# Stick-breaking attention: where a pair's queries are split, and how the query products are spread over the heads

## The chip, the cores and the metric

The kernel runs on one core of a Trainium2 chip. The metric is the device time in microseconds (us) of one execution. Five engines work from queues of their own, each strictly in the order in which the program lists its instructions: TensorE (PE, matrix products; its weight loads are shown as PEld), VectorE (DVE), ScalarE (ACT), GpSimd (POOL) and SyncE (SP), whose queue here issues the DMAs. Semaphores connect them: an instruction at the head of a queue waits for its inputs, and everything behind it on that queue waits too.

## The reference, cut to what matters

Two small transformer blocks run one after the other on 512 tokens of width 1024. The change touches only the attention of the second block, with 16 heads of 64 features:

```
q = split_heads(u @ attn_w_q[i])
o = stick_breaking_attention(q, k_shared, v_shared)
h = h + o @ attn_w_o[i]
...
z = einsum('bhqd,bhkd->bhqk', qb, kb) * scale
log_one_minus = where(causal, log_sigmoid(-z), 0)
log_remain = cumsum(log_one_minus, reverse) - log_one_minus
weights = where(causal, exp(log_sigmoid(z) + log_remain), 0)
out = einsum('bhqk,bhkd->bhqd', weights, vb)
```

## The kernel before, in words

All activations lie transposed, features on the partitions. A float32 product is made of three products of rounded halves (`mm3`): high by high, high by low, low by high. So every operand is split first: ScalarE (or VectorE) copies it into the rounded high half, VectorE subtracts that from the operand to get the low half.

The second block's attention is `stick()`. Two heads share 128 partitions, so heads go in eight pairs p = h // 2. The queries of pair p are one product of eight steps with a column block of `attn_w_q_2`; `q_out` scales the finished product into the tile `raw[p]` on VectorE (line 1272). `q_split` (lines 1282 to 1298) makes two stacked operands of it, one for each head: two copies on ScalarE (line 1287), two subtractions on VectorE (line 1294), and, as each operand holds its half once in each half of the partitions, four DMAs on SP's queue that copy 64 partitions to the other 64: the two high halves (line 1291), then the two low halves (line 1298). `k_split` (lines 1300 to 1306) does the keys with two ScalarE copies and two VectorE subtractions, without DMA.

For each head the work runs in this order. `scores` (L1318, mask L1322) multiplies keys by both query halves into PSUM, in the blocks B (768 columns, three key tiles) and A (512 columns, one key tile). ScalarE makes |z|, exp and ln of B and |z| and exp of A in `head_a` (lines 1327, 1328, 1331), and the ln of A in `head_b`. VectorE makes the softplus, adds up key tiles and splits it (`soft`, lines 1336 to 1342). TensorE adds the reversed cumulative sums into the same PSUM banks (`remain`, L1353: ten products for B, four for A), ScalarE takes the exponential of that (`weights`, L1360), and once for each pair `values` multiplies by the values (L594), whose result `y_split` splits on ScalarE (L275) and VectorE (L278).

The loop over h is pipelined by one head: iteration h issues `head_a(h + 1)`, that is the scores and the first functions of the next head, then `remain` and `weights` of head h. The two PSUM tiles of scores rotate, so `scores(h + 2)` waits for `weights(h)`.

Between these, `fill(n)` issues n steps of a generator `work()`: 39 steps of three 512-column products each. Step 1 is also where `raw[3]` is written. Steps 1 to 32 are the query products of pairs 4 to 7, eight steps each, all into one PSUM bank `wb`; with the last of its eight steps each issues its `q_out`, and the first step of the next one has to wait for that `q_out` to have read the bank. Steps 33 to 39 are the first seven steps of the output projection, which read y[0] to y[6] in turn. `FILL[h]` steps stand between `scores(h + 1)` and `remain(h)`, `FILL2[h]` steps at the end of iteration h, just ahead of `scores(h + 2)` in TensorE's queue. `self.ahead()`, also near the end of an iteration, splits the next weight block (ScalarE L214, VectorE L221) where the step before has taken one, and after every second block the next 1 MB weight load follows on SP's queue (L170).

Of the kernel before, what the change touches and what calls it, by code (L numbers as in the profile page):

```python
# [17 lines left out]
KT = 8  # L18
# [7 lines left out]
SQ = 4  # L26
PC = 3
COPIES = ("dada", "davv")
FILL = (1, 1, 1, 1, 0, 1, 1, 1, 1, 2, 1, 1, 0, 2, 1, 0)
FILL2 = (2, 1, 1, 2, 1, 3, 1, 3, 0, 2, 1, 3, 1, 2, 0, 3)  # L30
DUP = lambda nc: nc.vector.tensor_copy
KCUT = (0, 3, 6, 8)
CLIP = 256
# [62 lines left out]
class Kernel:  # L96
# [1161 lines left out]
    def stick(self):  # L1258
# [16 lines left out]
        def stacked(n):  # L1275
            return [self.tile("u", F32R) for _ in range(n)]

        def side(i):

            return slice(64 * i, 64 * i + 64), slice(64 - 64 * i, 128 - 64 * i)  # L1280

        def q_split(p, q):

            hi, lo = qs[p] = stacked(2), stacked(2)
            for i in range(2):
                r, other = side(i)
                nc.scalar.copy(hi[i][r], q[r])
                if p == 0:
                    nc.vector.tensor_copy(out=hi[i][other], in_=q[r])
                else:  # L1290
                    nc.sync.dma_start(hi[i][other].bitcast(F32), hi[i][r].bitcast(F32))
            for i in range(2):
                r, other = side(i)
                nc.vector.tensor_tensor(out=lo[i][r], in0=q[r], in1=hi[i][r].bitcast(F32), op=ALU.subtract)
                if p == 0:
                    nc.vector.tensor_tensor(out=lo[i][other], in0=q[r], in1=hi[i][r].bitcast(F32), op=ALU.subtract)
                else:
                    nc.sync.dma_start(lo[i][other].bitcast(F32), lo[i][r].bitcast(F32))

        def k_split(p):  # L1300

            ks[p] = stacked(2)
            for i in range(2):
                r, other = side(i)
                nc.scalar.copy(ks[p][i][r], self.K[p][r])
                nc.vector.tensor_tensor(out=ks[p][i][other], in0=self.K[p][r], in1=ks[p][i][r].bitcast(F32), op=ALU.subtract)
# [37 lines left out]
        def remain(h, ts):  # L1344

            o = z[h, len(ts)]
            own = [(t, t, self.tri) for t in ts]
            later = [(t + 1, t, self.rest if t > 0 else self.ones) for t in ts if t < 3]
            hi, lo = parts[h]
            for s, ops in ((hi, own), (hi, later), (lo, later), (lo, own)):  # L1350
                for t2, t, m in ops:
                    n, e = S - P * t2, OFF[S - P * t] + S - P * t - (S if t > 0 else 0)
                    nc.tensor.matmul(o[:, e - n : e], lhsT=m, rhs=s[:, OFF[n] : OFF[n] + n],  # L1353
                                     start=False, stop=s is lo and t2 == t, skip_group_check=True)

        def weights(h, c):
            if h not in wt:
                wt[h] = self.tile("b")
            n = c.stop - c.start
            nc.scalar.activation(wt[h][:, c], z[h, 1 if c is A else 3][:, 0:n], AF.Exp)  # L1360

        def head_a(h):

            sps[h] = self.tile("b")
            parts[h] = (self.tile("b", F32R), self.tile("b", F32R))
            scores(h, (1, 2, 3))
            scores(h, (0,))
            exps(h, B, z[h, 3][:, 0:768])
            ln(h, B)
            exps(h, A, z[h, 1])  # L1370

        def head_b(h):
            soft(h, B, z[h, 3][:, 0:768])
            ln(h, A)
            soft(h, A, z[h, 1])

        def values(p):
            self.pair_values(self.V[p], (wt.pop(2 * p), wt.pop(2 * p + 1)), vb)

        def y_split(p):  # L1380
            y[p] = self.split(vb)
# [7 lines left out]
        raw = {}  # L1389
# [34 lines left out]
        def fill(n):  # L1424
            for _ in range(n):
                next(steps, None)

        for h in range(NH):
            p = h // 2
            if h % 2 == 0 and 0 < p < KT - 1:  # L1430
                q_split(p + 1, raw.pop(p + 1))
                k_split(p + 1)
            if h + 1 < NH:
                head_a(h + 1)
            fill(FILL[h])
            remain(h, (1, 2, 3))
            remain(h, (0,))
            weights(h, B)
            if h + 1 < NH:
                head_b(h + 1)  # L1440
            weights(h, A)
            if h % 2 == 0 and p > 0:
                values(p - 1)
                y_split(p - 1)
            self.ahead()
            fill(FILL2[h])
            if h == NH - 2:
                ob = self.part(2)
                outs += [ob[:, 0:S], ob[:, S : 2 * S]]
                ws.append(self.take("attn_w_o_2", 1))  # L1450
                self.proj(outs[1], ws[1], y, 0, 6)
# [170 lines left out]
```

## Time and profile before

| | us |
|---|---|
| median of 3 runs | 2487.1 (2486.02 to 2488.62) |
| the profiled execution's own time | 2485.29 |
| its span, first to last instruction | 2483.5 |
| mean granted TensorE clock | 0.995 of full speed |
| stick(), from the first split of queries to the last steps of its first three output columns (1941.6 to 2083.6 in the span) | 142.0 |

The profiled execution is 1.81 us below the median of the runs, and 1.79 us of it lie outside the span. Rows of the timeline give the start and the length in us, the engine, the line of the kernel, the operation, the tile written and the tiles read, and, in brackets, how long the engine had been idle before and what released it. Entries are merged when they follow each other on one line; "x6" is six instructions.

### The profile page before, as it was taken

How to read it: one execution, taken by the hardware profiler on the slowest of the kernel's cores; microseconds unless marked ns; L12 is line 12 of the kernel's file. 1: busy time of each engine (PE TensorE's matmuls, PEld its weight loads, DVE VectorE, ACT ScalarE, POOL GpSimd, SP SyncE). 2: the span in 40 equal slices, each digit the busy share in tenths (PEclk: the TensorE clock that was granted, in tenths of full speed). 3: DMA queues.
4: the chain of work that ended last, by engine and by line, in shares of the span. 5: the costliest groups of instructions: out<-in, count | busy, mean ns of one | idle time of the engine just before them, and what ended most of it. 6: DMA issues, size and time to landing. Idle time of an engine off the chain costs nothing.

```text
span 2483.5 us, 29340 instructions
## 1 busy us (share of the span) xinstructions
PE 2442.0 (98%) x12060; PEld 2022.5 (81%) x12060; DVE 1364.6 (55%) x1917; ACT 911.0 (37%) x1298; POOL 173.9 (7%) x160
## 2 busy tenths in 40 slices
PE   8999999999999999899999999999999999999998
PEld 7887889877888886588888888888888777888887
DVE  7767575865443447874443444344445796444343
ACT  5335332553222335552222332222223795322232
POOL 2200110020000010330000010000001001000001
PEclk9999999999999999999999999999999999999999
DMA  4332323213223222313223222222222221322321
GB/s 171 96 114 82 106 104 120 90 69 110 96 97 113 85 102 89 96 54 106 94 97 113 85 102 99 93 94 102 94 102 85 72 73 51 106 94 100 113 85 68
DMA packets 51829, 237.42 MB, mean 96 GB/s; under 512 B 13168, under 2 KB 15600, under 8 KB 29808
## 3 DMA queue, kind: packets, MB, share of 16 engines
q1 hardware_dynamic: 51696, 235.55, 27.3%
q8 instruction: 95, 1.56, 0.3%
q14 instruction: 38, 0.31, 0.0%
HBM read 225.67 MB, written 2.13 MB: 92 GB/s over the span
## 4 chain that ended last, share of the span: by engine, by line
PE 86%; DVE 6%; ACT 3%; DMA 3%; issue 1%; POOL 0%; SPq 0%; DVEq 0%; ACTq 0%; POOLq 0%
PE bg L259 15%; PE bg L260 14%; PE bg L261 14%; PE mm L259 11%; PE mm L261 11%; PE mm L260 11%; DVE wl L221 2%; DMA d<-s 1%; PE part L259 1%; PE part L260 1%; PE part L261 1%; PE mm L594 1%; PE mm L1009 1%; DMA u<-d 1%; PE bg L576 1%
## 5 line engine op out<-in xcount | busy, mean ns | idle before, releaser
L221 DVE TENSOR_TENSOR wl<-raw,wh 128x1024 fp32r<-128x1024 f32 (+1 forms) x406 | 495.0, 1245 | 176.1 <-ACT wh L214 173.4
L259 PE MATMUL bg<-xg,wh 128*128 128x512 f32 x1440 | 562.0, 390 | 6.9 <-ACT wh L198 4.6
L260 PE MATMUL bg<-xg,wh 128*128 128x512 f32 x1440 | 560.8, 389 | 0.5 <-DVE xg L286 0.5
L261 PE MATMUL bg<-xg,wl 128*128 128x512 f32 x1440 | 560.9, 389 | 0.3 <-DVE wl L199 0.3
L214 ACT CAST wh<-raw 128x1024 fp32r<-128x1024 f32 (+1 forms) x406 | 403.1, 1029 | 398.4 <-PE mm L260 215.4
L259 PEld LDWEIGHTS bg<-xg,wh 128*128 128x128 f32 x1440 | 270.7, 188 | 64.7 <-ACT wh L198 5.1
L260 PEld LDWEIGHTS bg<-xg,wh 128*128 128x128 f32 x1440 | 270.7, 188 | 57.1 <-DVE xg L286 1.0
L261 PEld LDWEIGHTS bg<-xg,wl 128*128 128x128 f32 x1440 | 270.5, 188 | 56.9 <-DVE wl L199 0.7
L873 DVE TENSOR_TENSOR u<-bg,u 128x512 f32<-128x512 f32 x88 | 60.8, 691 | 381.6 <-PE bg L261 361.4
L874 ACT ACTIVATE u<-u 128x512 f32<-128x512 f32 x88 | 55.7, 633 | 560.0 <-DVE u L873 560.0
L259 PE MATMUL mm<-b,wh 128*128 128x512 f32 (+1 forms) x672 | 260.6, 388 | 0.0
L261 PE MATMUL mm<-b,wl 128*128 128x512 f32 (+1 forms) x672 | 260.6, 388 | 0.0
L260 PE MATMUL mm<-b,wh 128*128 128x512 f32 (+1 forms) x672 | 260.6, 388 | 0.0
L300 POOL TENSOR_TENSOR u<-u,u 128x512 f32<-128x512 f32 x61 | 82.7, 1360 | 1794.1 <-ACT u L298 1793.6
L464 DVE SCALAR_TENSOR_TENSOR x<-mm,x 128x512 f32<-128x512 f32 x111 | 76.5, 689 | 210.6 <-PE mm L261 210.6
L259 PE MATMUL mm<-xg,wh 128*128 128x512 f32 x400 | 159.7, 399 | 1.5 <-ACT b L1328 1.3
L261 PE MATMUL mm<-xg,wl 128*128 128x512 f32 x400 | 156.3, 391 | 0.0
L260 PE MATMUL mm<-xg,wh 128*128 128x512 f32 x400 | 156.3, 391 | 0.0
L259 PEld LDWEIGHTS mm<-b,wh 128*128 128x128 f32 x672 | 126.2, 188 | 25.9
L260 PEld LDWEIGHTS mm<-b,wh 128*128 128x128 f32 x672 | 126.2, 188 | 25.9
L261 PEld LDWEIGHTS mm<-b,wl 128*128 128x128 f32 x672 | 126.1, 188 | 25.8
L259 PE MATMUL mm<-u,wh 128*128 128x512 f32 x248 | 97.6, 394 | 0.6 <-DVE u L1236 0.6
(255 smaller groups left out, 3442.0 us busy)
## 6 DMA issues: line engine op xcount, KB each, us to landing
raw<-w SPq DMA_DIRECT2D x171, 1024.0 KB, 4.8
raw<-w SPq DMA_DIRECT2D x32, 896.0 KB, 4.6
b<-dec SPq DMA_DIRECT2D x8, 640.0 KB, 7.1
u<-relb SPq DMA_DIRECT2D x16, 256.0 KB, 5.1
u<-d SPq DMA_DIRECT2D x14, 256.0 KB, 5.9
u<-u SPq DMA_DIRECT2D x28, 128.0 KB, 2.2
b<-b SPq DMA_DIRECT2D x32, 66.0 KB, 2.0
x<-x SPq DMA_DIRECT2D x8, 256.0 KB, 5.6
```

The source lines that it names most:

```text
L214: nc.scalar.copy(hi[:, s], raw[:, s])
L221: self.nc.vector.tensor_tensor(out=lo[:, s], in0=raw[:, s], in1=hi[:, s].bitcast(F32), op=ALU.subtract)
L259: nc.tensor.matmul(out, lhsT=a[0], rhs=b[0], start=start, stop=False)
L260: nc.tensor.matmul(out, lhsT=a[0], rhs=b[1], start=False, stop=False)
L261: nc.tensor.matmul(out, lhsT=a[1], rhs=b[0], start=False, stop=stop)
L300: eng.tensor_tensor(out=acc, in0=acc, in1=sq, op=ALU.add)
L464: nc.vector.scalar_tensor_tensor(out=x, in0=ps, scalar=scale, in1=x, op0=ALU.mult, op1=ALU.add)
L576: self.nc.tensor.transpose(o[:, d0 : d0 + P], p[:, s0 : s0 + P], self.ident)
L594: self.nc.tensor.matmul(o[r, P * t : S], lhsT=v[:, t, r], rhs=pt[i][:, OFF[n] : OFF[n] + n], start=t == 0, stop=t == 3)
L873: nc.vector.tensor_tensor(out=a, in0=o[:, 0:S], in1=self.rb, op=ALU.mult)
L874: nc.scalar.activation(a, a, AF.Silu)
L1009: nc.tensor.matmul(o[32 * g : 32 * g + 32], lhsT=d[j + g], rhs=q[g][:, x0 : x0 + t.stop - t.start], start=j == 0, stop=j == n - 4)
```

## The change

`q_split` of the next pair moves, in the iterations of heads 2, 4, ..., 12, from the start of the iteration to a place behind `weights(h, A)` of that iteration, ahead of `values` and `y_split`. And the two lists that spread the steps of `work()` over the heads get other numbers.

```
-FILL = (1, 1, 1, 1, 0, 1, 1, 1, 1, 2, 1, 1, 0, 2, 1, 0)
-FILL2 = (2, 1, 1, 2, 1, 3, 1, 3, 0, 2, 1, 3, 1, 2, 0, 3)
+FILL = (1, 1, 1, 1, 0, 1, 1, 1, 1, 2, 1, 1, 0, 2, 0, 0)
+FILL2 = (3, 2, 2, 2, 1, 3, 1, 3, 1, 3, 0, 0, 1, 2, 1, 3)
...
         for h in range(NH):
             p = h // 2
             if h % 2 == 0 and 0 < p < KT - 1:
-                q_split(p + 1, raw.pop(p + 1))
                 k_split(p + 1)
             if h + 1 < NH:
                 head_a(h + 1)
...
                 head_b(h + 1)
             weights(h, A)
+            if h % 2 == 0 and 0 < p < KT - 1:
+                q_split(p + 1, raw.pop(p + 1))
             if h % 2 == 0 and p > 0:
                 values(p - 1)
                 y_split(p - 1)
```

Counted from the lists, the steps that end a query product (8, 16, 24, 32) fall before into `FILL` of head 3, `FILL` of head 6, `FILL` of head 9 and `FILL2` of head 11; after, into `FILL` of head 2, `FILL2` of head 5 (its first of three), `FILL2` of head 7 (its last) and `FILL` of head 10. Step 39, the one that reads y[6], falls before into `FILL2` of head 15; after, into `FILL2` of head 14.

## Rows read from the trace of the kernel before

**Rows 1.** The page's first part: busy time of TensorE in the whole span.
```profile
PE 2442.0 (98%) x12060; PEld 2022.5 (81%) x12060; DVE 1364.6 (55%) x1917; ACT 911.0 (37%) x1298; POOL 173.9 (7%) x160
```

**Rows 2.** Windows of stick(): length, busy time of each engine, granted clock, DMA.
```profile
core 0: us, PE busy (x) PEld busy (x) DVE busy (x) ACT busy (x) POOL busy (x), PEclk, DMA share, GB/s
1963.20:2039.90 76.70, 74.60 (x445) 59.31 (x445) 72.51 (x115) 75.12 (x116) 0.00 (x0) 1.00 0.19 50
...
2053.00:2056.00 3.00, 3.00 (x9) 2.41 (x9) 2.50 (x5) 2.78 (x4) 0.00 (x0) 0.54 0.00 0
```

**Rows 3.** ScalarE's timeline in stick(); L1327 on 768 columns opens a head.
```profile
1963.22 0.81 ACT L1327 ACTIVATE b<-part 128x768 f32<-128x768 f32 x1 [2.11 <-PE part L1322]
...
1971.10 0.81 ACT L1327 ACTIVATE b<-part 128x768 f32<-128x768 f32 x1
...
1972.82 0.84 ACT L1331 ACTIVATE b<-b 128x768 f32<-128x768 f32 x1
...
1976.95 0.81 ACT L1327 ACTIVATE b<-part 128x768 f32<-128x768 f32 x1
...
1982.27 1.25 ACT L1287 CAST u<-u 64x512 fp32r<-64x512 f32 x2
...
1984.83 0.81 ACT L1327 ACTIVATE b<-part 128x768 f32<-128x768 f32 x1
...
1990.60 1.07 ACT L214 CAST wh<-raw 128x1024 fp32r<-128x1024 f32 x1
...
2044.44 1.26 ACT L1287 CAST u<-u 64x512 fp32r<-64x512 f32 x2 [4.36 <-DVE u L1272]
...
2053.16 0.81 ACT L1327 ACTIVATE b<-part 128x768 f32<-128x768 f32 x1 [0.26 <-PE part L1322]
...
2061.00 0.82 ACT L1327 ACTIVATE b<-part 128x768 f32<-128x768 f32 x1 [0.57 <-PE part L1322]
...
2072.22 1.46 ACT L1360 ACTIVATE b<-part 128x768 f32<-128x768 f32 x2 [4.93 <-PE part L1353]
```

**Rows 4.** VectorE's timeline: softplus, a pair's splits, a scaled query product.
```profile
1973.72 0.96 DVE L1336 SCALAR_TENSOR_TENSOR b<-part,b 128x768 f32<-128x768 f32 x1
...
1978.76 0.68 DVE L278 TENSOR_TENSOR u<-mm,u 128x512 fp32r<-128x512 f32 x1
...
1984.98 1.40 DVE L1294 TENSOR_TENSOR u<-u,u 64x512 fp32r<-64x512 f32 x2
...
2043.72 0.68 DVE L1272 SCALAR_TENSOR_TENSOR u<-mm,u 128x512 f32<-128x512 f32 x1
```

**Rows 5.** TensorE's timeline: scores, steps of the generator, cumulative sums, values.
```profile
1962.00 0.85 PE L1318 MATMUL part<-u,u 128*128 128x384 f32 x5 [0.36 <-DMA u<-u]
...
2003.27 0.50 PE L259 MATMUL mm<-xg,wh 128*128 128x512 f32 x1 [0.16 <-DVE u L1272]
...
2051.47 1.02 PE L1318 MATMUL part<-u,u 128*128 128x384 f32 x6 [3.91 <-ACT b L1360]
...
2056.26 2.24 PE L1353 MATMUL part<-b,c 128*128 128x384 f32 x14
...
2059.71 0.92 PE L1318 MATMUL part<-u,u 128*128 128x384 f32 x6
...
2062.12 2.24 PE L1353 MATMUL part<-b,c 128*128 128x384 f32 x14
...
2066.59 0.50 PE L259 MATMUL part<-u,wh 128*128 128x512 f32 x1
...
2070.82 2.23 PE L1353 MATMUL part<-b,c 128*128 128x384 f32 x14
...
2074.35 2.37 PE L594 MATMUL mm<-b,u 128*64 128x512 f32 x16
```

**Rows 6.** SP's queue, and issue to landing of the low query halves' copies.
```profile
1971.60 1.41 SPq L1298 DMA_DIRECT2D u<-u x2
...
DMA to landing us min/median/max: 2.2/2.2/6.0
```

More of the change, by code (lines that the diff above doesn't have):

```diff
@@ L28 @@
 COPIES = ("dada", "davv")
-FILL = (1, 1, 1, 1, 0, 1, 1, 1, 1, 2, 1, 1, 0, 2, 1, 0)
-FILL2 = (2, 1, 1, 2, 1, 3, 1, 3, 0, 2, 1, 3, 1, 2, 0, 3)
+FILL = (1, 1, 1, 1, 0, 1, 1, 1, 1, 2, 1, 1, 0, 2, 0, 0)
+FILL2 = (3, 2, 2, 2, 1, 3, 1, 3, 1, 3, 0, 0, 1, 2, 1, 3)
 DUP = lambda nc: nc.vector.tensor_copy
@@ L1430, in stick @@
             if h % 2 == 0 and 0 < p < KT - 1:
-                q_split(p + 1, raw.pop(p + 1))
                 k_split(p + 1)
@@ L1441, in stick @@
             weights(h, A)
+            if h % 2 == 0 and 0 < p < KT - 1:
+                q_split(p + 1, raw.pop(p + 1))
             if h % 2 == 0 and p > 0:
```

## The prediction

> **What bounds the kernel now.** The first thing read is the page's busy times [rows 1]: TensorE 98% of the span. That is true of the feed-forward stages and says nothing about this one, so the next view is the windows of stick() alone. From 1963.20 to 2039.90, the part in which the loop runs evenly, TensorE has work in 74.60 of 76.70 us, but ScalarE in 75.12 and VectorE in 72.51 [rows 2]. Three engines are full at once, and the timelines say which of them leads. On ScalarE the first |z| of head 3 starts at 1971.10, of head 4 at 1976.95, of head 5 at 1984.83 [rows 3], and in this stretch no entry of ScalarE follows idle time. The short interval (5.85 us) leads from an odd head to the next pair's even one, the long one (7.88 us) from an even head to its odd partner; in the long one ScalarE also has the two query copies (1.25 us, at 1982.27) and the two key copies. So ScalarE's instruction count sets the pace, with hardly any slack around it. A wait put in front of a |z| is paid in full: ScalarE has nothing else that it may do, since its queue is in order.
>
> One wait is already there: at 2044.44 the query copies of the last pair begin after 4.36 us of idle ScalarE, released by `q_out` (L1272) [rows 3], which stands on VectorE at 2043.72 [rows 4]. Step 32 ends that pair's product only in `FILL2` of head 11, so its `q_out` is queued behind the whole softplus of head 12.
>
> **What is removed.** After the change step 32 falls into `FILL` of head 10, and `q_split` no longer stands ahead of the odd head's |z|. The 4.36 us go. And each long interval that holds a `q_split` loses its 1.25 us of copies: 7.88 becomes about 6.62. No instruction is removed: ScalarE copies, VectorE subtractions, the 24 DMAs of six moved splits and 39 steps are all issued still, in other places.
>
> **What the moved split waits for.** This is the term that decides. The operands that `q_split(p + 1)` makes in iteration 2p are read by `scores(2p + 2)`, the first thing TensorE does in iteration 2p + 1. Before, the split stood a whole head earlier. Now its low halves stand on VectorE behind `soft(2p + 1)`, and must then go through SP's queue. From the |z| of the odd head to the |z| of the next even head the chain is:
> - |z|, exp, ln of B on ScalarE, to VectorE's first softplus instruction: 1971.10 to 1973.72, 2.62 us [rows 3, 4];
> - the softplus of both blocks, to the instruction behind it: 1973.72 to 1978.76, 5.04 us [rows 4];
> - the first of the two low-half subtractions: half of 1.40, 0.70 us [rows 4];
> - its DMA: SP issued the two low copies of an earlier pair from 1971.60, and such a copy lands 2.2 us (median) after its issue [rows 6];
> - from the landing to the |z|: the score products released by that DMA went at 1962.00, and the |z| of that head began at 1963.22 [rows 5, 3], 1.22 us.
>
> Sum 11.78 us, where the short interval was 5.85. The high half is no later: its copies follow `weights(h, A)` on ScalarE, while VectorE is still in the softplus. The lower bound of the DMA is 2.2 and the upper 6.0, the longest row, which a copy took that followed a 1 MB weight load. By the lists the load that comes near a split is issued in iteration 8, behind the low copies, so I take 2.2.
>
> **What the moved steps wait for.** Step 16 ends the product of pair 5. Its `q_out` is now issued in `FILL2` of head 5, behind `soft(6)`, and steps 17 and 18 stand directly behind it and ahead of `scores(7)`. Step 17 must wait for that `q_out`. The trace of before shows this wait in small (0.16 us at 2003.27 [rows 5]). From |z| of head 6 to |z| of head 7 it makes 2.62 + 5.04 + 0.68 (`q_out`) + 1.41 (two steps of 0.705, from the six between 2066.59 and 2070.82 [rows 5]) + 1.29 (scores at 2059.71 to |z| at 2061.00 [rows 5, 3]) = 11.04 us in place of 6.62. At step 25 (ahead of the cumulative sums of head 8) the wait is for work that these sums need too; it is taken at nothing, and at 0.7, one `q_out`, in the range. The extra steps in heads 0 to 2 lie where TensorE waited for DMA or weights anyway; if that cover is gone they cost 0.7 each.
>
> **The weight copies** (1.07 us each [rows 3]) fall by the new steps into iterations 3, 6, 8, 11. In 6 and 8 the new wait of the |z| hides them; in 3 and 11 they add to the intervals of heads 5 and 13.
>
> **The sum over heads 2 to 15.** Before: |z| of head 2 at 1963.22, of head 15 at 2061.00 [rows 3], 97.78 us. After: six short intervals of 11.78 (70.7) and seven long ones: six of 6.62, two of them with 1.07 more, and one of 11.04 (52.9). 123.6 us, so +25.8. It contains the gone 4.36.
>
> **The tail.** Step 39 reads y[6] and now stands in iteration 14, ahead of six output steps and of `remain(15)`. y[6]'s low half is queued behind `soft(15)`: |z| of head 15 + 2.62 + 5.04 + 0.68 = 8.34, then seven steps (4.94) and 1.40 from the cumulative sums to the weights (2070.82 to 2072.22) = 14.68 us, where it was 11.22 [rows 3, 5]: +3.46. Step 39 no longer stands between these sums and the last values; weights ended at 2073.68 (2072.22 + 1.46) and the values started at 2074.35 [rows 3, 5], so 0.67 comes back: +2.8.
>
> **The clock.** After its only long wait (3.91 us, at 2051.47) TensorE ran at a granted 0.54 from 2053 to 2056 [rows 5, 2], the lower level of 1.2 GHz for nearly all of it. Scores and two steps then took 4.79 us (to 2056.26) against 2.41 + 0.70 at the full clock (2059.71 to 2062.12, plus a step): 1.68 us, of which the |z| saw 0.40 (1.69, 2051.47 to 2053.16, against 1.29). By the chain above two new TensorE waits are as long, ahead of `scores(6)` (4.3 us) and of step 17 (4.4); I charge 0.40 for the first and 1.68 for the second, where steps stand ahead of the scores. The wait at head 14 exists before as after. +2.1.
>
> **Sum:** 25.8 + 2.8 + 2.1 = +30.7. Against the profiled execution's 2485.29 that is 2516.0; the median of the runs lies 1.81 higher, so 2518.
>
> **Rivals.**
> 1. *The clock falls after every new wait.* The waits ahead of scores 4, 8, 10, 12, of step 25 and of step 39 are 1 to 3.4 us by the same walk. Each would cost 0.40 to 1.68 more: +2.4 to +10.1, up to 2528. Against it: in the even part TensorE was idle for 2.10 us in all (76.70 - 74.60), and the granted clock stayed at 1.00 [rows 2]. The Trainium skill ("TensorE: Matmul & The Clock Gate", "HAM oscillation") says that in a loop whose matmul bursts are parted by waits the array falls to half rate again in every round. By that rule this rival's 2528 holds, by the row above 2518.
> 2. *Only the split costs.* If `q_out` of pair 5 and y[6] come early enough, the step moves are free: 4.4, 2.8 and 1.7 drop out, 2509. VectorE would have to run the softplus out of the list's order; nothing in the trace does.
> 3. *Faster.* The split is in time: the copies' 1.25 us only pass from the long interval to the short one (5.85 + 1.25 = 7.10), and the gone 4.36 us are the whole effect: 2482.7, with the tail's 2.8 still 2485.5. It decides from the point where the low half lands within 7.10 - 1.22 = 5.9 us of the odd head's |z|. The chain needs 11.78 - 1.22 = 10.6 to there; the 5.04 us of softplus ahead of the subtraction would have to be out of it. The list puts them in.
> 4. *No effect*, should the list not be the order of the queues. In the trace all queues follow it.
>
> **How the numbers follow.** 0.74 for the forecast (2510 to 2525), 0.12 for rival 1, 0.08 for rival 2, 0.04 for rival 3, 0.02 for rival 4. The unknown ends are the clock (+10), the DMA (+3.8 for one late copy) and, downwards, waits that overlap. The range that leaves out no more than 2 in 10 is 2505 to 2529. About 0.2% (5 us) is what a measurement can tell from no change; the first three cases are all slower by more: 0.94, same 0.03, faster 0.03.
>
> **What would show it.** In the profile after: a wait of ScalarE of 3.5 to 5 us ahead of the |z| of heads 4, 6, 8, 10, 12 and 14, ended by TensorE's scores, and these ended by a DMA; no idle time ahead of the last pair's query copies; a wait of 4 us for `q_out` ahead of step 17; `remain(15)` 3 us later after the last |z|. If the |z| of even heads still follow the odd ones by about 6 us, the chain is wrong and with it the sum.

## The result and the profile after

The changed kernel takes 2529.49 us (median of 4 runs, 2528.95 to 2531.24), the kernel before 2487.84: ratio 1.0171, 95% interval 1.0159 to 1.0183. It is slower by 41.7 us; 30.2 were forecast (2518 against the 2487.8 of before), and the time lies just beyond the upper end of the range, 2529.

The profiled execution took 2528.95 us, 43.7 more than the one of before. The windows of the loop, first from |z| of head 3 to |z| of head 15, then around the wait and the work of head 6:

```profile
core 0: us, PE busy (x) PEld busy (x) DVE busy (x) ACT busy (x) POOL busy (x), PEclk, DMA share, GB/s
1970.70:2099.80 129.10, 99.01 (x499) 78.56 (x498) 87.12 (x136) 84.18 (x128) 0.00 (x0) 0.84 0.15 41
...
2000.00:2003.20 3.20, 0.41 (x1) 0.19 (x1) 2.26 (x4) 0.00 (x0) 0.00 (x0) 0.82 0.55 126
2003.20:2005.40 2.20, 2.16 (x9) 2.19 (x10) 0.00 (x0) 0.08 (x1) 0.00 (x0) 0.50 0.10 23
2005.40:2009.60 4.20, 4.20 (x17) 3.72 (x17) 1.61 (x3) 3.57 (x6) 0.00 (x0) 0.59 0.00 0
2009.60:2016.50 6.90, 4.29 (x23) 3.46 (x23) 5.28 (x9) 2.92 (x6) 0.00 (x0) 1.00 0.00 0
```

Three engines were full in this loop before [rows 2]; now ScalarE works 84 of 129 us. And the granted clock, 0.98 before from head 3 to head 15, is 0.84 over the loop: the scores of head 6 run at 0.50, the lower level. So do those of the other five even heads:

```profile
1982.00:1984.10 2.10, 2.10 (x9) 2.10 (x10) 0.00 (x0) 0.07 (x1) 0.00 (x0) 0.50 0.03 8
2027.20:2029.40 2.20, 2.16 (x9) 2.19 (x10) 0.18 (x1) 0.08 (x1) 0.00 (x0) 0.50 0.02 5
2048.20:2050.30 2.10, 2.09 (x9) 2.10 (x10) 0.21 (x1) 0.01 (x1) 0.00 (x0) 0.50 0.56 115
2069.70:2071.80 2.10, 2.10 (x9) 2.10 (x10) 0.00 (x0) 0.02 (x1) 0.00 (x0) 0.50 0.05 13
2090.20:2092.30 2.10, 2.08 (x9) 2.10 (x10) 0.00 (x0) 0.00 (x0) 0.00 (x0) 0.50 0.03 7
```

ScalarE's timeline:

```profile
1970.67 0.81 ACT L1327 ACTIVATE b<-part 128x768 f32<-128x768 f32 x1
...
1984.03 0.81 ACT L1327 ACTIVATE b<-part 128x768 f32<-128x768 f32 x1 [6.19 <-PE part L1322]
...
1992.57 0.81 ACT L1327 ACTIVATE b<-part 128x768 f32<-128x768 f32 x1
...
2005.32 0.81 ACT L1327 ACTIVATE b<-part 128x768 f32<-128x768 f32 x1 [5.58 <-PE part L1322]
...
2016.48 0.81 ACT L1327 ACTIVATE b<-part 128x768 f32<-128x768 f32 x1 [3.96 <-PE part L1322]
...
2084.61 1.25 ACT L1287 CAST u<-u 64x512 fp32r<-64x512 f32 x2
...
2099.81 0.81 ACT L1327 ACTIVATE b<-part 128x768 f32<-128x768 f32 x1 [1.51 <-PE part L1322]
...
2115.68 1.46 ACT L1360 ACTIVATE b<-part 128x768 f32<-128x768 f32 x2 [9.98 <-PE part L1353]
```

Heads 3 to 4 take 13.36 us where it was 5.85, heads 5 to 6 12.75; head 6 to 7, the interval with step 17, 11.16. ScalarE's waits ahead of the six even heads are 4.5 to 6.2 us, somewhat longer than the 3.5 to 5 that were to show the chain. The last pair's query copies (2084.61) wait for nothing now. Who holds the scores back stands first on TensorE's timeline of the changed kernel:

```profile
1978.96 0.41 PE L1318 MATMUL part<-u,u 128*128 128x384 f32 x1 [1.75 <-DMA u<-u]
1981.95 1.41 PE L1318 MATMUL part<-u,u 128*128 128x384 f32 x5 [2.58 <-DMA u<-u]
...
2000.82 0.41 PE L1318 MATMUL part<-u,u 128*128 128x384 f32 x1 [3.01 <-DMA u<-u]
2003.24 1.40 PE L1318 MATMUL part<-u,u 128*128 128x384 f32 x5 [2.01 <-DMA u<-u]
...
2013.69 0.50 PE L259 MATMUL mm<-xg,wh 128*128 128x512 f32 x1 [2.61 <-DVE u L1272]
```

The copies that released the scores of head 6, on SP's queue, the high halves (L1291) and the low (L1298):

```profile
1998.52 1.10 SPq L1291 DMA_DIRECT2D u<-u  x2
2000.94 1.15 SPq L1298 DMA_DIRECT2D u<-u  x2
```

And what stood ahead of these low halves on VectorE, from the first softplus instruction of head 5 on:

```profile
1995.17 0.96 DVE L1336 SCALAR_TENSOR_TENSOR b<-part,b 128x768 f32<-128x768 f32 x1 [0.71 <-ACT b L1331]
...
2000.20 1.40 DVE L1294 TENSOR_TENSOR u<-u,u 64x512 fp32r<-64x512 f32 x2
```

For head 6 the chain reads: |z| of head 5 at 1992.57, softplus at 1995.17 (2.60 later), low halves at 2000.20 (5.03), issue at 2000.94 (0.74), scores released at 2003.24 (2.30), |z| at 2005.32 (2.08). Four of the five terms are those of the forecast to within 0.1 us. The last was put at 1.22. And TensorE waits twice within one set of scores: first for the high halves' copy, then, one product later, for the low halves': 3.01 + 2.01 us.

Summed over all heads (from the starts of L1327 on 768 columns; the last column is the |z| of head 15 to `weights(15)`):

| kernel | six short intervals | seven long ones | head 2 to 15 | tail |
|---|---|---|---|---|
| before | 37.20 | 60.58 | 97.78 | 11.22 |
| forecast, without its 2.1 of clock | 70.7 | 52.9 | 123.6 | 14.68 |
| after | 77.54 | 58.19 | 135.73 | 15.87 |

Of the 43.7 us in the profile, 37.95 lie between heads 2 and 15, 4.65 in the tail up to the weights, and 0.86 ahead of head 2, 0.75 of them already ahead of head 0, where nothing was moved.

### The profile page after: what moved, and what is told of

Its sections match the earlier page's. It is cut to its first block, busy times and chain, and to the rows that moved or that the text cites. A ratio compares the mean times of both kernels' runs of the same rounds, so it can differ in the third digit from the quotient of the medians.

```text
span 2527.2 us, 29361 instructions
## 1 busy us (share of the span) xinstructions
PE 2460.0 (97%) x12060; PEld 2037.2 (81%) x12060; DVE 1365.8 (54%) x1917; ACT 911.5 (36%) x1298; POOL 174.0 (7%) x160
## 4 chain that ended last, share of the span: by engine, by line
PE 87%; DVE 6%; ACT 3%; DMA 3%; issue 2%; POOL 0%; SPq 0%; DVEq 0%; ACTq 0%; POOLq 0%
PE bg L259 15%; PE bg L260 15%; PE bg L261 15%; PE mm L259 11%; PE mm L260 11%; PE mm L261 11%; DVE wl L221 1%; PE part L259 1%; PE part L260 1%; PE part L261 1%; PE part L1318 1%; DMA u<-u 1%; PE mm L1009 1%; DMA d<-s 1%; PE bg L576 1%
```

## The experiments

The theory after this reading: the chain and the step waits are as forecast, and what is missing is a TensorE clock that falls in all six waits, not in one. The rival: the chain itself is longer than its rows, or the two lists cost more than was worked out.

**The two parts alone.** e1_move has the new place of the split and the old lists, e2_lists the new lists and the old place.

```
e1_move:  -                q_split(p + 1, raw.pop(p + 1))      (start of iteration)
          +                q_split(p + 1, raw.pop(p + 1))      (behind weights(h, A))
e2_lists: -FILL = ... -FILL2 = ...   +FILL = ... +FILL2 = ...  (as in the change)
```

> Only the move of the split; the two lists as before. If the low halves' chain (ScalarE 2.6, softplus 5.0, subtraction 0.7, DMA 2.2, scores 1.2 us) and a TensorE clock that falls in each of the six waits are the cause, the six intervals from an odd head's |z| to the next even head's are 12.5 to 13 us as in the changed kernel, and the time is about 2520 (2488 + 22.6 of waits + some 10 of clock). If the lists carry most of the loss, the time stays under 2500.

> Only the two lists; the split stands where it stood before. By the chain for step 17 (4.4 us), the tail (2.8) and the gone 4.36 us wait: 2491 to 2496, short intervals still about 6 us. If the lists carry most of the loss: over 2510.

e1_move: 2522.04 us, ratio 1.0129 (1.0112 to 1.0146), +32.9 on its 2489.19. Its short intervals are 12.74 to 12.88 us. e2_lists: 2500.67 us, ratio 1.0047 (1.0032 to 1.0062), +11.5. So the move is most of the loss, and the two add up to 44.4 where both together cost 41.7. The lists alone cost more than the 2 to 7 us expected. The largest single piece of the excess is a wait that the changed kernel doesn't have: heads 5 to 6 take 10.17 us where it was 6.71. The tail is 16.05 us where 14.68 were forecast, and heads 7 to 8 and 9 to 10 take 1.8 and 2.0 more than before. In e2_lists, TensorE's timeline at the scores of head 6 and at step 17:

```profile
1997.00 2.12 PE L1318 MATMUL part<-u,u 128*128 128x384 f32 x6 [4.49 <-DMA u<-u]
...
2008.16 0.50 PE L259 MATMUL mm<-xg,wh 128*128 128x512 f32 x1 [3.34 <-DVE u L1272]
```

And SP's queue in e2_lists ahead of that, with the weight load (L170):

```profile
1989.66 0.33 SPq L170 DMA_DIRECT2D raw<-w  x1
1990.10 1.10 SPq L1291 DMA_DIRECT2D u<-u  x2
1991.29 1.21 SPq L1298 DMA_DIRECT2D u<-u  x2
```

The lists move a weight load into the end of iteration 3. With the split in its old place, at the start of iteration 4, the copies are issued 0.44 us behind that 1 MB, and TensorE waits 4.49 us for them ahead of the scores of head 6. In the changed kernel the split stands a head later: there the load was issued at 1993.05 and the first copy at 1998.52.

**The clock, held up.** e3_warm is the changed kernel with idle products ahead of the six scores; e6_move_warm is the same on e1_move; e8_warm17 adds 16 ahead of step 17.

```
+WARM = {4: 16, 6: 18, 8: 14, 10: 14, 12: 18, 14: 22}
+            for _ in range(WARM.get(h, 0) if len(ts) == 3 else 0):
+                nc.tensor.matmul(o[:, 0:S], lhsT=self.identr, rhs=k, start=True, stop=True, ...)
e8_warm17, ahead of step 17:
+                        for _ in range(16):
+                            nc.tensor.matmul(vb, lhsT=self.identr, rhs=ks[3][0], start=True, stop=True)
```

> The changed kernel with 14 to 22 more products of 512 columns ahead of the scores of heads 4, 6, ..., 14; they write the bank that the scores then start anew, so nothing is computed from them, and they only keep TensorE at work during its wait. Clock theory (a clock fallen to half in all six waits carries what the forecast missed): granted clock 1.00 in those scores, short intervals near 11.8 in place of 12.8, long ones shorter too, time 2515 to 2521. Rival (the DMA or the queues are slower than the rows said): intervals as in the changed kernel, 2529 or more.

> Only the move, with the idle products of e3_warm ahead of the six scores (they compute nothing). Clock theory: short intervals 11.9 to 12.5, from head 2 to head 15 about 121 us where the move alone has 131; time some 10 us under the move alone (2522), about 2511. Rival (the clock matters only where the lists add waits): within 3 us of the move alone.

> e3_warm with 16 more idle products ahead of step 17, into the bank of the values, which the values start anew. Clock theory: the interval from head 6 to head 7 falls from 12.7 to 11.0 us, as the forecast's chain has it without the clock, and the time by 1.5 to 2 us. Rival (that interval's wait is something else): it stays at 12.7.

e3_warm: 2525.06 us, ratio 1.0142 (1.0127 to 1.0157); e6_move_warm: 2513.00 us, ratio 1.0094 (1.0078 to 1.0109); e8_warm17: 2522.50 us, ratio 1.0129 (1.0116 to 1.0143). The scores of head 4 in e3_warm, by windows:

```profile
1981.95:1984.10 2.15, 2.15 (x14) 1.98 (x15) 0.00 (x0) 0.93 (x2) 0.00 (x0) 1.00 0.06 13
```

TensorE's timeline of e3_warm around them (L1317 the idle products, L1321 the scores):

```profile
1977.05 3.89 PE L1317 MATMUL part<-u,c 128*128 128x512 f32 x16
1980.78 0.34 PE L1321 MATMUL part<-u,u 128*128 128x384 f32 x1
1981.95 0.82 PE L1321 MATMUL part<-u,u 128*128 128x384 f32 x5 [0.83 <-DMA u<-u]
```

The release by the DMA comes at 1981.95, as without the idle products, but the five score products take 0.82 us in place of 1.41, at a granted 1.00. The adding of work to a waiting engine made the kernel faster:

| kernel | short | long | head 2 to 15 | tail |
|---|---|---|---|---|
| e1_move | 76.79 | 54.42 | 131.21 | 11.22 |
| e6_move_warm | 72.79 | 47.08 | 119.87 | 11.22 |
| after | 77.54 | 58.19 | 135.73 | 15.87 |
| e3_warm | 72.97 | 54.75 | 127.72 | 16.04 |
| e8_warm17 | 72.99 | 53.89 | 126.88 | 14.46 |

The granted clock over the loop of e1_move and of e6_move_warm:

```profile
1970.00:2100.00 130.00, 104.22 (x529) 83.55 (x529) 90.78 (x142) 89.61 (x137) 0.00 (x0) 0.84 0.15 41
1978.00:2090.00 112.00, 105.96 (x598) 85.20 (x594) 83.53 (x130) 82.46 (x127) 0.00 (x0) 1.00 0.18 48
```

In the loops of the profiled executions the clock is 11.3 us of the move alone (1.9 for each of six waits) and 8.0 of the changed kernel; in the medians of the whole time it is 9.0 and 4.4. e3_warm's expectation of 2515 to 2521 was missed by 4 us, for two reasons. Its interval from head 6 to 7 grew from 11.16 to 12.72, since TensorE now waited 4.31 us ahead of step 17 and the clock fell there. And its profiled execution gives 2.8 us back behind the attention: from `weights(15)` to the end it takes 414.4 us, the changed kernel 411.5, with a TensorE wait of 2.25 us at 2170.91 where the changed kernel has 0.96. What lengthens that wait the runs don't show.

TensorE at step 17, in e3_warm and in e8_warm17:

```profile
2011.12 0.58 PE L260 MATMUL mm<-xg,wh 128*128 128x512 f32 x1 [4.31 <-DVE u L1273]
...
2015.12 0.40 PE L260 MATMUL mm<-xg,wh 128*128 128x512 f32 x1
```

e8_warm17 fills that wait too and has 11.82 from head 6 to 7, where 11.0 were expected. The 16 products ran on to 2015.12, where `q_out` had ended at 2014.30, and that is the 0.8 between. Its time is 2.6 us under e3_warm's, more than the 1.5 to 2 expected, but not for the reason given: in the profiled executions the loop is only 0.8 us shorter; the tail, which the 16 products do not touch, is 1.6 shorter (see the last section).

**The chain ahead of the low halves.** e4_between is the changed kernel with the split between the softplus of B and that of A; e9_high_early leaves the high halves' copies and DMAs at the start of the iteration and moves only the low halves.

```
e4_between, in the place of head_b(h + 1):
+                soft(h + 1, B, z[h + 1, 3][:, 0:768])
+                if h % 2 == 0 and 0 < p < KT - 1:
+                    q_split(p + 1, raw.pop(p + 1))
+                ln(h + 1, A)
+                soft(h + 1, A, z[h + 1, 1])
e9_high_early:
+                q_high(p + 1, raw[p + 1])           (start of iteration, ahead of k_split)
...
-                q_split(p + 1, raw.pop(p + 1))
+                q_low(p + 1, raw.pop(p + 1))        (behind weights(h, A))
```

> The changed kernel with the split issued between the softplus of block B and that of block A of the next head, so that 1.8 us of softplus leave the chain ahead of the low halves. If VectorE's order decides: each of the six short intervals 1.8 us shorter, time about 2519. Rival (the ScalarE copies or the high halves' DMA decide): no change, 2529.

> The changed kernel with the high halves (ScalarE copies and their DMAs) issued where they stood before, and only the low halves' subtractions and DMAs in the new place. If the chain through the softplus to the low halves decides: short intervals 12.5 to 13 us as in the changed kernel, the long ones 1.25 us longer, time 2530 to 2537. Rival (the high halves' copies and DMAs, for which TensorE waits first, decide): short intervals fall by 2 us or more, time under 2520.

e4_between: 2517.99 us, ratio 1.0120 (1.0102 to 1.0139). Its six short intervals sum to 65.96 against 77.54, 1.93 less each, where 1.8 of softplus had left the chain. But this edit also brings the high halves forward (their first copy is issued at 1975.13 where it was 1976.62), so it does not part the low halves from the high ones. e9_high_early does: 2536.87 us, ratio 1.0186 (1.0172 to 1.0200). Its short intervals (76.52) are those of the changed kernel, though the high halves went out a head earlier; the long ones grew by 6.6 in sum. TensorE's timeline at the scores of head 4 (L1327 is the line of the scores in this kernel) shows the first product without a wait and all of it ahead of the second:

```profile
1981.60 0.33 PE L1327 MATMUL part<-u,u 128*128 128x384 f32 x1
1987.18 1.41 PE L1327 MATMUL part<-u,u 128*128 128x384 f32 x5 [5.25 <-DMA u<-u]
```

So the low halves behind the softplus decide, and the high halves, for which TensorE waits first, do not.

**The wait that the change was rid of, alone.** e5_step32 is the kernel before, the split in its old place, with step 32 ahead of the softplus of head 12.

```
-FILL = (1, 1, 1, 1, 0, 1, 1, 1, 1, 2, 1, 1, 0, 2, 1, 0)
-FILL2 = (2, 1, 1, 2, 1, 3, 1, 3, 0, 2, 1, 3, 1, 2, 0, 3)
+FILL = (1, 1, 1, 1, 0, 1, 1, 1, 1, 2, 1, 2, 0, 2, 1, 0)
+FILL2 = (2, 1, 1, 2, 1, 3, 1, 3, 0, 3, 2, 0, 1, 2, 0, 3)
```

> The kernel before with steps 30 to 32 a little earlier (one more step in FILL of head 11, in FILL2 of heads 9 and 10, none in FILL2 of head 11), the split left in its old place. Theory: the 4.36 us wait of ScalarE ahead of the last pair's query copies goes, and with it the one fall of the clock; 2483 to 2485 where before has 2488. Rival: TensorE's own work fills the end of the stage, so the wait only moves there and the time stays.

2484.81 us against 2489.99, ratio 0.9976 (0.9966 to 0.9985): 5.2 us faster than before, and faster than the changed kernel. The windows of e5_step32, all of stick() and the place where the wait was:

```profile
1941.60:2083.00 141.40, 136.02 (x776) 107.63 (x775) 121.34 (x189) 117.37 (x179) 0.00 (x0) 1.00 0.20 58
2035.00:2060.00 25.00, 24.30 (x146) 18.91 (x145) 24.06 (x40) 23.47 (x36) 0.00 (x0) 1.00 0.25 72
```

The interval from head 12 to 13, 12.37 us with the wait, is 7.88, and the clock stays at 1.00. From head 2 to 15 it takes 93.10 us where it was 97.78.

## Why the prediction was right in its direction and short in its size

- **The chain to the low halves** was right, term by term (2.60, 5.03, 0.74, 2.30 against 2.62, 5.04, 0.70, 2.2). With the clock held up, the short intervals are 11.85 to 12.55 us where 11.78 was forecast. In the changed kernel the 0.6 more of heads 3 to 4 has a row: a `q_out` (0.69 us, at 1973.27) stands ahead of that softplus. The 2.1 us that six such intervals run over in e6_move_warm are small beside the rest; where they come from was not followed up.
- **The gone wait** was right: 4.36 us, and e5_step32 shows what it is worth by itself, with the one fall of the clock: 5.2 us, 4.7 of them between heads 2 and 15.
- **Step 17** was right as a chain, 11.04 forecast, 11.02 measured when the overrun of 0.8 is taken off e8_warm17's 11.82. In the changed kernel TensorE, still slow from head 6, reached it late and waited only 2.61 us, not 4.4, and the clock did not fall there: the 1.68 charged for it was not paid. e3_warm, where TensorE came there at the full clock, has the forecast's wait (4.31) and an interval of 12.72, the 11.04 and the 1.68 together.
- **The tail** was forecast as 14.68, and was 15.87 with a fallen clock, 14.46 in e8_warm17, where it held.
- **The clock is the step that failed.** The prediction counted as long only "two new TensorE waits", and put those ahead of scores 4, 8, 10 and 12 at 1 to 3.4 us. The walk that gave these waits is not in the prediction. The low halves came when its chain says (TensorE was released 10.67 us after the |z| of head 5, 10.56 by the chain), but TensorE had come to its wait earlier: first it waited for the high halves, then, one product later, about 2 us more for the low ones. Together the waits ahead of scores 4, 6, 8, 10, 12 and 14 are 4.33, 5.02, 3.79, 3.73, 4.41 and 6.08 us, and all six let the clock fall. Its price was off too: 0.40 us to the |z|, from a row of before at which the clock fell only midway (0.54 came after the scores' first products, [rows 2, 5]). Scores that run wholly at 0.50 cost 0.86 (2.08 against 1.22), and the steps and `remain` behind them are slow too (0.59 from 2005.40 to 2009.60): 1.9 us for each wait, 11.3 for the move. The forecast charged 2.1 in all.
- **What is left.** The profile's +43.7 is 13.0 us over the forecast's +30.7. In e8_warm17 the loop is 8.9 us shorter than in the changed kernel and the tail 1.4: 10.3 of clock where 2.1 were charged, 8.2 of the 13.0. Between heads 2 and 15 e8_warm17 is still 3.3 over the 123.6: 2.3 in the six short intervals and 0.8 by its own overrun. The rest is 0.86 ahead of head 2 and small differences behind the weights.
- So **rival 1**, with 12 in 100 given to it, came nearest: the clock fell ahead of all six scores and in step 39, though not at step 17. It had its 2528 from the same too-short waits and the same low price. The Trainium skill's rule ("TensorE: Matmul & The Clock Gate", "HAM oscillation") that a loop of waits loses the clock anew in every round is what the changed kernel shows: 0.50 in each of the six scores.
- **Rivals 2 to 4** fell: the lists cost 11.5 us by themselves, and the split was not in time in any head.

## What to carry to other kernels

Where several engines are full at once, an operand must be ready a whole round before its reader, not behind the long work of the same round: count the full chain from the place where its last piece is issued, DMA included, to the first reader. Count waits with only one short product between them as one wait: here such pairs let the clock fall in all six rounds of the changed kernel, and the work behind them took up to twice as long for some microseconds; idle products in the waiting place show how much of a loss that is. And a wait of a few microseconds at one place is mended at that place: here three steps of a list, not the order of the loop.

## What the runs showed of the hardware that was not expected

Waits of the same length need not end alike. At step 39 TensorE waited 0.99 and, one product later, 1.93 us in the changed kernel and in e8_warm17. Afterwards the clock was at 0.51 in the one and at 1.00 in the other. The window behind the wait in the changed kernel:

```profile
2108.00:2111.30 3.30, 3.11 (x7) 2.48 (x8) 0.13 (x1) 0.00 (x0) 0.00 (x0) 0.51 0.00 0
```

The window behind it in e8_warm17:

```profile
2103.00:2110.00 7.00, 7.00 (x37) 5.76 (x35) 0.00 (x0) 1.37 (x3) 0.00 (x0) 1.00 0.00 0
```

That is 1.4 us of the tail (15.87 against 14.46) from one place. Of the six kernels whose lists put step 39 there, only e8_warm17 kept the clock; the tails of the other five are 15.87 to 16.09 us. The same was seen ahead of the scores of head 6: after a wait of 1.75 us in both, the clock was 1.00 in e3_warm (2001.50 to 2003.60) and fell in e8_warm17 (0.61 from 2005.70 to 2010.00). What decides it the runs don't tell.
